# Measured transfer latencies in the scheduler, norm columns asked for from POOL's queue, and another order of inputs in the first output projection

## The chip, the cores and the metric

The kernel runs on one core of one Trainium2 chip. The metric is the device time of one execution in microseconds (us). A core has five engines that matter here, each with its own queue of instructions that it works off in order: TensorE (PE, matrix products), VectorE (DVE), ScalarE (ACT), GpSimd (POOL) and SyncE (SP), which in this kernel only asks for transfers. Engines wait for each other through semaphores.

## What is computed

A two-layer encoder over 512 positions of width 1024, in float32. Layer 0 mixes the positions with four heads of differential attention and four heads of a gated linear attention (HGRN2, both directions); layer 1 mixes them with a spatial gating unit. After each mixer comes a SwiGLU feed-forward network (FFN), and at the end a norm. The part that the change touches, from the reference:

```python
def even_mixer(h, w_in, w_out, lam, lambda_init, subln, rel_bias, lb_fwd, lb_bwd, hg_norm):
    da_q, da_k, da_v, hg_q, hg_zf, hg_zb, hg_i, hg_g = jnp.split(h @ w_in, ...)
    o_a = diff_attention(da_q, da_k, da_v, lam, rel_bias)          # heads 0 to 3
    o_a = rms_norm(o_a, subln) * (1.0 - lambda_init)
    o_b = hgrn2_bidir(silu(hg_q), hg_zf, hg_zb, hg_i, lb_fwd, lb_bwd)  # heads 4 to 7
    o_b = rms_norm(o_b, hg_norm) * silu(hg_g)
    return jnp.concatenate([o_a, o_b], axis=-1) @ w_out

# layer 0: h = h + even_mixer(rms_norm(h)); layer 1: h = h + odd_mixer(rms_norm(h))
# both:    h = h + swiglu(rms_norm(h)); at the end rms_norm(h)
```

## The kernel before

Activations lie transposed, features on the 128 partitions and the 512 positions along a row, so that a 128x512 tile is the unit of nearly all work. Each product is made of three matmuls: an operand is split into a rounded part and the rest (whi and wlo for weights, ph and pl for attention weights, vdh and vdl for values), and high x high, high x low and low x high are added. The rounded part is made by ACT, the rest by DVE, from a weight `raw` that a DMA brought.

The names that matter: `o_a` is the weighted sum of values of one attention head (four chunks of three matmuls each, from ph, pl, vdh, vdl); `pt` are transposes of the attention weights `pr`, which come from `e`, scaled on POOL; `or_b` is a gated linear head before its norm and `on` after it; `or_a` is an attention head before its norm; `g` is the gate's projection; `oe` the first output projection, with one group oe0 to oe7 for each 128 output features, and eight inputs k: attention heads for k = 0 to 3 (`oa`), gated heads for k = 4 to 7 (`ob`).

A norm over features needs, for each position, a sum over partitions. `rnorm` (lines 440 to 459) makes it: PE sums into a row (`st`), ACT copies the row (`ln`), a small DMA lays it over partitions (`ms`), POOL adds the epsilon and takes the power -1/2 (`rr`), a small DMA writes it to DRAM (`dr`), and a DMA reads it back as `R`, 128x512, the same row on each partition (256 KB). DVE then multiplies with R. There are eight such norms: gated heads b0 to b3, attention heads a0 and a1, and the norm in each of the two FFNs (f0, f1); the other norms go without the transfers. `bt` is the bias of an attention head, 448 KB.

The order of all instructions is not written by hand. `Plan.schedule` (line 110 and on) simulates five engines, with a cost for each operation and a latency after which its users may start (`LATENCY`, and 2.0 for a DMA, line 196), takes at each step the operation with the lowest priority number that is ready and has its buffers, and so emits one order. On the chip each engine works off its part of that order as it stands. All transfers are asked for by SP.

`out_proj` (line 883) makes the first two groups of the projection with all inputs but the last one, then gives them the last one, and makes the other six groups one after the other.

Of the kernel before, what the change touches and what calls it, by code (L numbers as in the profile page):

```python
# [16 lines left out]
P = 128  # L17
S = 512
# [8 lines left out]
LATENCY = 0.25  # L27
# [36 lines left out]


class Op:
    __slots__ = ("eng", "cost", "fn", "bufs", "prio", "deps", "users", "ready", "start", "table", "seq", "alt", "port")


class Plan:  # L70
# [6 lines left out]
    def buf(self, kind, name, dt=F32, shape=None):  # L77
        return Buf(self, kind, name, dt, shape)

    def op(self, eng, cost, fn, outs=(), ins=(), after=(), table=None, prio=None, alt=None, port=None):  # L80
        o = Op()
        o.port = eng == "POOL" if port is None else port
        o.alt = alt
        o.eng, o.cost, o.fn, o.table = eng, cost, fn, table
        o.seq = len(self.ops)
        if prio is None:
            prio = o.seq
            if self.base is not None:
                self.base += 1e-3
                prio = self.base  # L90
        o.prio = prio
        o.deps, o.users, o.bufs = set(after), [], set()
        for views, w in ((ins, False), (outs, True)):
            for v in views:
                if not isinstance(v, (View, Buf)):
                    continue
                b = v if isinstance(v, Buf) else v.buf
                part = None if isinstance(v, Buf) else v.part
                o.bufs.add(b)
                for q, qp, qw in b.log:  # L100
                    if (w or qw) and meets(part, qp):
                        o.deps.add(q)
                b.log.append((o, part, w))
        o.deps.discard(o)
        for b in o.bufs:
            b.left += 1
        self.ops.append(o)
        return o

    def schedule(self):  # L110
# [5 lines left out]
        table = None  # L116
        port = 0.0
# [6 lines left out]
        events = []  # L124
        n = 0
# [11 lines left out]
        while events:  # L137
# [15 lines left out]
            for e in engines:  # L153
# [39 lines left out]
                order.append(o)  # L193
                n += 1
                idle[e] = t + cost
                lat = 2.0 if e == "DMA" else LATENCY
                heapq.heappush(events, (t + cost, 2 * n, "near", o))
                heapq.heappush(events, (t + cost + lat, 2 * n + 1, "done", o))
        if len(order) != len(self.ops):
            left = [o for o in self.ops if o not in set(order)]  # L200
            raise RuntimeError("stuck: " + ", ".join(
# [6 lines left out]
def use(x):  # L208
    if isinstance(x, Buf):
        return x.ap()  # L210
    return x.get() if isinstance(x, View) else x
# [3 lines left out]
def encoder_kernel(  # L215
# [21 lines left out]
    nc = tc.nc  # L237
# [45 lines left out]
    def blk(ap, i):  # L283
        return ap[:, i * P:(i + 1) * P]

    def dma(o, i, kb, prio=None, after=()):
        return plan.op("DMA", max(kb / 360.0, 0.45), lambda: nc.sync.dma_start(use(o), use(i)), [o], [i], after=after, prio=prio)

    def inside(*xs):
        for x in xs:  # L290
# [149 lines left out]
    def rnorm(sq, n, name, kind):  # L440
        pr = buf("trn", f"sp_{name}", F32R)
        acopy(row(pr, 0), sq)
        vtt(row(pr, 1), sq, frow(pr, 0), ALU.subtract, either=True)
        ps = buf("aux", f"st_{name}")
        first = ps(lambda ap: ap[0:1])
        mms(ps, [(first, onesr[:, 0:1], row(pr, 0), True, False), (first, onesr[:, 0:1], row(pr, 1), False, True)])
        line = buf("tmp", f"ln_{name}")
        act(line(lambda ap: ap[0:1]), first, AF.Copy, scale=1.0 / n, cost=0.5)
        c, r = buf("ms", f"ms_{name}"), buf("rr", f"rr_{name}")
        dma(c, line(lambda ap: ap[0:1]), 20)  # L450
        gts(c, c, 1.0, EPS, cost=0.1)
        gtt(r, c, mhalf, ALU.pow, cost=1.1)
        dr = dp.tile([1, S], F32, name=f"dr_{name}")
        o = dma(dr.rearrange("o (p j) -> (o p) j", j=NB), r, 20)
        R = buf(kind, f"R_{name}")
        dma(R, dr.broadcast_to([P, S]), 256, after=[o])
        return R

    def operands(b, name):
# [295 lines left out]
    def da(h, q, k, base, vals):  # L755
# [3 lines left out]
        rows = um[h]  # L759
        src = bass.AP(rows.tensor, rows.offset + P - 1, [[D - 1, P], [1, 896]])  # L760
        o = plan.op("DMA", 1.3, lambda: nc.sync.dma_start(bt.ap(), src), [bt], after=[op_um] + after)
        QK, Kl = buf("huge", f"QK_{h}", F32R), buf("big", f"Kl_{h}", F32R)
        lo, hi = slice(0, 64), slice(64, 128)
        A64, V64 = 0.52, 0.6
# [118 lines left out]
    def out_proj(w, mx, order, early, name, nrm):  # L883
        group = [(buf("acc", f"{name}{d}"), weight(w[d])) for d in range(early)]
        for part in (order[:-1], order[-1:]):
            for d, (ps, wt) in enumerate(group):
                for k in part:
                    chunk2(ps, wt, k, mx[k], k == order[0], k == order[-1])
        for d, (ps, wt) in enumerate(group):
            residual(d, ps, nrm)  # L890
        for d in range(early, KC):
            ps, wt = buf("acc", f"{name}{d}"), weight(w[d])
            for k in order:
                chunk2(ps, wt, k, mx[k], k == order[0], k == order[-1])
            residual(d, ps, nrm)
# [136 lines left out]
        return gs, n, wts, one, out  # L1032

    n1 = Norm(1, "f0")
    out_proj(woe, mix, [0, 1, 4, 5, 2, 6, 7, 3], 2, "oe", n1.add)
    n2 = Norm(2, "m1")
    gs, n, wts, one, out_pair = ffn(0, n1, "a", n2.add, after=[da_end[3]])
    for dq in range(KC // 2):
# [183 lines left out]
```

## Time and profile before

| | |
|---|---|
| three runs | 1175.45, 1178.22, 1175.07 us (median 1175.45) |
| the profiled execution | 1179.28 us; its span from first to last instruction 1177.5 us |
| TensorE's mean granted clock | 0.996 of full speed |
| busy: PE, DVE, ACT, POOL | 98%, 78%, 49%, 12% of the span |

The profile is one execution. Busy time is the share of the span in which an engine runs an instruction. An engine that is not the bottleneck may stand idle at no cost; what counts here is where PE stands and which other engine, transfer or queue it stands for. The three runs lie within 3.15 us of each other.

### The profile page before, as it was taken

The numbers are of one execution on the slowest core, as the hardware profiler recorded it, in microseconds if no ns is written. First come the engines' busy times: TensorE is split into PE (matmuls) and PEld (weight loads), VectorE is DVE, ScalarE is ACT, GpSimd is POOL, SyncE is SP. The second block draws the span as 40 slices with busy tenths as digits, with TensorE's granted clock in tenths as the row PEclk, the third lists the DMA queues.
The fourth block names the chain that finished last, engine by engine and source line by source line (L and its number), as shares of the span: only waits on it lengthen the run. The fifth ranks groups of instructions, "written<-read, shape, count | busy, mean of one in ns | idle before, by whom it ended". The sixth has DMA issues, their size and how long they took to land.

```text
span 1177.5 us, 17613 instructions
## 1 busy us (share of the span) xinstructions
PE 1151.4 (98%) x7072; PEld 1029.9 (87%) x7072; DVE 915.8 (78%) x1335; ACT 577.9 (49%) x881; POOL 142.3 (12%) x146
## 2 busy tenths in 40 slices
PE   7999998999999999999999999999999999999997
PEld 5888887778889999999999888888999999999996
DVE  6776796788878987878887745659899777778775
ACT  5444546667555544444444542345555444444434
POOL 1672765223000000000000000000000000000000
PEclk9999999999999999999999999999999999999998
DMA  6612303225213322324231433331433242423202
GB/s 239 201 52 45 116 17 98 51 98 199 88 22 149 122 94 77 140 72 144 72 123 56 162 90 90 90 125 36 153 108 107 73 143 72 144 72 112 104 1 72
DMA packets 27978, 118.58 MB, mean 101 GB/s; under 512 B 5204, under 2 KB 7380, under 8 KB 19704
## 3 DMA queue, kind: packets, MB, share of 16 engines
q1 hardware_dynamic: 27896, 117.46, 29.9%
q8 instruction: 55, 0.90, 0.3%
q14 instruction: 27, 0.22, 0.1%
HBM read 115.30 MB, written 4.23 MB: 102 GB/s over the span
## 4 chain that ended last, share of the span: by engine, by line
PE 91%; DMA 4%; DVE 3%; POOL 1%; ACT 1%; issue 1%; SPq 0%; POOLq 0%; DVEq 0%; ACTq 0%
PE fo_0b L329 8%; PE fo_0a L329 8%; PE uo L329 4%; PE oe L329 4%; PE oo L329 4%; PE vo L329 4%; PE lv L655 2%; PE q L329 2%; PE zf L329 2%; PE vi L329 2%; PE zb L329 2%; PE fo_18a L329 2%; PE last L329 2%; PE g L329 2%; PE dq L329 1%; PE o_a L329 1%
## 5 line engine op out<-in xcount | busy, mean ns | idle before, releaser
L298 DVE TENSOR_TENSOR wlo<-raw,whi 128x1024 fp32r<-128x1024 f32 (+1 forms) x65 | 82.2, 1269 | 9.4 <-ACT whi L317 8.8
L298 DVE TENSOR_TENSOR lb<-comb,hb 128x1024 fp32r<-128x1024 f32 x44 | 53.7, 1221 | 38.5 <-ACT hb L317 38.5
L317 ACT CAST hb<-comb 128x1024 fp32r<-128x1024 f32 x44 | 46.1, 1048 | 61.2 <-PE pb6a L946 2.4
L298 DVE TENSOR_TENSOR la<-raw,ha 128x1024 fp32r<-128x1024 f32 x44 | 53.8, 1224 | 27.0 <-ACT ha L317 26.7
L317 ACT CAST ha<-raw 128x1024 fp32r<-128x1024 f32 x44 | 46.2, 1049 | 52.4 <-PE pa10a L946 2.4
L317 ACT CAST whi<-raw 128x1024 fp32r<-128x1024 f32 (+1 forms) x65 | 66.4, 1032 | 4.2 <-DMA raw<-we 2.6
L298 DVE TENSOR_TENSOR l<-raw,h 128x1024 fp32r<-128x1024 f32 (+1 forms) x48 | 54.5, 1135 | 16.5 <-ACT h L317 14.9
L317 ACT CAST hc<-comb 128x1024 fp32r<-128x1024 f32 x44 | 46.2, 1050 | 39.7 <-PE fo_0b L329 15.5
L317 ACT CAST h<-raw 128x1024 fp32r<-128x1024 f32 (+1 forms) x48 | 46.7, 976 | 29.4 <-PE pb6a L946 2.0
L298 DVE TENSOR_TENSOR comb<-comb,raw 128x512 f32<-128x512 f32 x88 | 60.2, 684 | 0.1
L298 DVE TENSOR_TENSOR lc<-comb,hc 128x1024 fp32r<-128x1024 f32 x44 | 53.6, 1218 | 3.8 <-ACT hc L317 3.8
L922 DVE TENSOR_TENSOR comb<-raw 128x1024 f32<-128x1024 f32 x44 | 53.6, 1218 | 0.0
L685 POOL TENSOR_TENSOR W<-W,T 128x512 f32<-128x512 f32 x37 | 47.6, 1297 | 48.2 <-PE lv L655 43.0
L310 POOL TENSOR_TENSOR rr_m<-ms_m,mhalf 128x4 f32<-128x4 f32 x2 | 4.6, 2302 | 346.0 <-DVE ms_m L306 346.0
L310 POOL TENSOR_TENSOR rr_fin<-ms_fin,mhalf 128x2 f32<-128x2 f32 x2 | 1.4, 696 | 336.7 <-DVE ms_fin L306 336.7
L329 PE MATMUL vo<-whi,x_m 128*128 128x512 f32 x128 | 40.3, 391 | 0.1
L329 PE MATMUL uo<-x_m,whi 128*128 128x512 f32 x128 | 40.1, 394 | 0.0
L329 PE MATMUL oo<-mx,whi 128*128 128x512 f32 x128 | 39.5, 390 | 0.0
L317 ACT CAST hd<-raw 128x512 fp32r<-128x512 f32 x44 | 27.4, 622 | 21.4 <-PE pa0b L946 2.0
L659 DVE COPY_PREDICATED att<-maskt,lv 128x512 f32<-128x512 uint8 x28 | 20.7, 740 | 17.1 <-PE lv L655 14.7
L648 ACT COPY km<-W 128x512 f32<-128x512 f32 x28 | 18.6, 663 | 30.5 <-POOL W L685 10.3
L655 PEld LDWEIGHTS lv<-W,km 128*128 128x128 f32 x224 | 30.5, 191 | 2.3
(2621 smaller groups left out, 4201.1 us busy)
## 6 DMA issues: line engine op xcount, KB each, us to landing
raw<-wfi SPq DMA_DIRECT2D x44, 1024.0 KB, 5.0
raw<-wfo SPq DMA_DIRECT2D x20, 1024.0 KB, 5.0
raw<-we SPq DMA_DIRECT2D x24, 512.0 KB, 5.4
raw<-wev SPq DMA_DIRECT2D x8, 512.0 KB, 5.9
raw<-woe SPq DMA_DIRECT2D x8, 512.0 KB, 4.4
raw<-wov SPq DMA_DIRECT2D x8, 512.0 KB, 4.9
raw<-wo SPq DMA_DIRECT2D x8, 512.0 KB, 3.7
raw<-woo SPq DMA_DIRECT2D x8, 512.0 KB, 3.7
```

What stands on the lines that cost most here:

```text
L298: return plan.op("DVE", cost, lambda: V.tensor_tensor(use(o), use(a), use(b), op), [o], [a, b], prio=prio, after=after, alt=alt, port=insi ...
L310: return plan.op("POOL", cost, lambda: G.tensor_tensor(use(o), use(a), use(b), op), [o], [a, b], prio=prio)
L317: return plan.op("ACT", cost, lambda: A.copy(use(o), use(a)), [o], [a], prio=prio)
L329: T.matmul(use(o), lhsT=use(l), rhs=use(r), start=s0, stop=s1)
L648: plan.op("ACT", 0.52, lambda km=km, s=s: A.copy(km.ap().rearrange("p (n two s) -> p n two s", two=2, s=s), mixed(1, 0, S, s)(W.ap())), [k ...
L655: T.matmul(blk(ps.ap(), b), lhsT=blk(km.ap(), b), rhs=mixed(0, b * P, P, s)(W.ap()), start=True, stop=True)
L659: plan.op("DVE", 0.6, lambda ps=ps, li=li: V.copy_predicated(att.ap().rearrange("p (b c) -> p b c", b=NB), maskt[:, li:li + 1].broadcast_t ...
L685: return lambda: eng.tensor_tensor(view(W.ap()), view(W.ap()), fn(TT.ap()), ALU.mult)
L922: plan.op("DVE", 1.14, lambda: V.tensor_tensor(comb.ap()[:, 0:2], raw.ap()[:, 0:1].broadcast_to([P, 2, S]), raw.ap()[:, 1:3], ALU.add), [c ...
```

## The change

Three things are changed. Each operation of the plan has a latency of its own (`lat`), which is as before except for four kinds of transfers: ms 1.5, dr 1.0, R 4.5 and bt 5.0 in place of 2.0. The eight R transfers are issued by `nc.gpsimd` (POOL's queue) instead of `nc.sync` (SP's). And the first output projection takes its inputs in the order 4, 5, 6, 7, 0, 1, 2, 3.

```diff
 class Op:
-    __slots__ = ("eng", "cost", "fn", "bufs", "prio", "deps", "users", "ready", "start", "table", "seq", "alt", "port")
+    __slots__ = ("eng", "cost", "fn", "bufs", "prio", "deps", "users", "ready", "start", "table", "seq", "alt", "port", "lat")
...
+        o.lat = 2.0 if eng == "DMA" else LATENCY
...
-                lat = 2.0 if e == "DMA" else LATENCY
-                heapq.heappush(events, (t + cost + lat, 2 * n + 1, "done", o))
+                heapq.heappush(events, (t + cost + o.lat, 2 * n + 1, "done", o))
...
-    def dma(o, i, kb, prio=None, after=()):
-        return plan.op("DMA", max(kb / 360.0, 0.45), lambda: nc.sync.dma_start(use(o), use(i)), [o], [i], after=after, prio=prio)
+    def dma(o, i, kb, prio=None, after=(), q=nc.sync):
+        return plan.op("DMA", max(kb / 360.0, 0.45), lambda: q.dma_start(use(o), use(i)), [o], [i], after=after, prio=prio)
...
-        dma(c, line(lambda ap: ap[0:1]), 20)
+        dma(c, line(lambda ap: ap[0:1]), 20).lat = 1.5
...
         o = dma(dr.rearrange("o (p j) -> (o p) j", j=NB), r, 20)
+        o.lat = 1.0
         R = buf(kind, f"R_{name}")
-        dma(R, dr.broadcast_to([P, S]), 256, after=[o])
+        dma(R, dr.broadcast_to([P, S]), 256, after=[o], q=G).lat = 4.5
...
         o = plan.op("DMA", 1.3, lambda: nc.sync.dma_start(bt.ap(), src), [bt], after=[op_um] + after)
+        o.lat = 5.0
...
-    out_proj(woe, mix, [0, 1, 4, 5, 2, 6, 7, 3], 2, "oe", n1.add)
+    out_proj(woe, mix, [4, 5, 6, 7, 0, 1, 2, 3], 2, "oe", n1.add)
```

What the change does to the order is seen at three places. In the rows below, the number right behind a name is that of the head, block or weight, and the last number that of the buffer.

The first place is DVE's queue around the norm of gated head b2, whose R is R_b2; on2 is the normed head, and pl_0 and vdl belong to attention head 0. Before:

```order
L298 TENSOR_TENSOR pl_0_1670<-pt2_0_1592,ph_0_1661 128x512
L298 TENSOR_TENSOR wlo25_1686<-raw25_1412,whi25_1677 128x1024
L302 SCALAR_TENSOR_TENSOR on2_1695<-or_b2_1530,colt_81,R_b2_1664 128x512
L659 COPY_PREDICATED att3_1282<-maskt_87,lv64_3_1679 128x512
L298 TENSOR_TENSOR pl_0_1670<-pt3_0_1603,ph_0_1661 128x512
L302 SCALAR_TENSOR_TENSOR vdl_1724<-vd0_1397,rr_m0_295,vdh_1709 128x512
L771 TENSOR_TENSOR QK_1_1717<-dqr1_1459,QK_1_1717 64x512
L302 SCALAR_TENSOR_TENSOR vdl_1724<-vd1_1403,rr_m0_295,vdh_1709 128x512
L302 SCALAR_TENSOR_TENSOR vdl_1724<-vd2_1476,rr_m0_295,vdh_1709 128x512
L302 SCALAR_TENSOR_TENSOR vdl_1724<-vd3_1545,rr_m0_295,vdh_1709 128x512
```

The same place of DVE's queue in the order of the change:

```order
L298 TENSOR_TENSOR pl_0_1674<-pt2_0_1611,ph_0_1662 128x512
L298 TENSOR_TENSOR pl_0_1674<-pt3_0_1615,ph_0_1662 128x512
L660 COPY_PREDICATED att3_1315<-maskt_87,lv32_3_1683 128x512
L686 TENSOR_TENSOR W_3_1201<-W_3_1201,T_3_1181 128x16x32
L302 SCALAR_TENSOR_TENSOR vdl_1708<-vd0_1395,rr_m0_295,vdh_1698 128x512
L302 SCALAR_TENSOR_TENSOR vdl_1708<-vd1_1402,rr_m0_295,vdh_1698 128x512
L302 SCALAR_TENSOR_TENSOR vdl_1708<-vd2_1469,rr_m0_295,vdh_1698 128x512
L302 SCALAR_TENSOR_TENSOR on2_1727<-or_b2_1515,colt_81,R_b2_1656 128x512
L302 SCALAR_TENSOR_TENSOR vdl_1708<-vd3_1523,rr_m0_295,vdh_1698 128x512
L298 TENSOR_TENSOR wlo26_1741<-raw26_1572,whi26_1725 128x1024
```

All four pl_0 and three of the four vdl now stand ahead of on2, and a weight's split (wlo26) behind the last vdl; before, the last pl_0 and all four vdl stood behind on2.

The second place is POOL's queue around the norm of gated head b3 (ms_b3, rr_b3, R_b3), with e2_1 and e3_1 of attention head 1. Before:

```order
L313 TENSOR_SCALAR ms_b3_1896<-ms_b3_1896 128x4
L313 TENSOR_SCALAR e2_1_1877<-e2_1_1877,rs2_1_1918 128x512
L310 TENSOR_TENSOR rr_b3_1943<-ms_b3_1896,mhalf_84 128x4
L313 TENSOR_SCALAR e3_1_1907<-e3_1_1907,rs3_1_1969 128x512
L779 MEMSET Kl_2_1998 64x512
L780 MEMSET Kl_2_1998 64x512
L313 TENSOR_SCALAR e0_2_2071<-e0_2_2071,rs0_2_2110 128x512
```

The same place of POOL's queue in the order of the change:

```order
L313 TENSOR_SCALAR e2_1_1896<-e2_1_1896,rs2_1_1934 128x512
L313 TENSOR_SCALAR ms_b3_1929<-ms_b3_1929 128x4
L310 TENSOR_TENSOR rr_b3_1961<-ms_b3_1929,mhalf_84 128x4
L781 MEMSET Kl_2_1972 64x512
L782 MEMSET Kl_2_1972 64x512
L287 DMA R_b3_1994<-dr_b3_107 128x512
L313 TENSOR_SCALAR e3_1_1936<-e3_1_1936,rs3_1_2008 128x512
```

R_b3 is now asked for here, and e3_1 stands behind it; e2_1 went ahead of ms_b3.

The third place is PE's queue at the end of attention: the transposes of the last part of attention head 3 (pr3_3), and o_a3. Before:

```order
L817 MATMUL pt0_3_2412<-ident_82,pr3_3_2497 128x128
L817 MATMUL pt1_3_2442<-ident_82,pr3_3_2497 128x128
L817 MATMUL pt2_3_2458<-ident_82,pr3_3_2497 128x128
L817 MATMUL pt3_3_2462<-ident_82,pr3_3_2497 128x128
L329 MATMUL g3_2492<-x_m02_139,whi31_2303 128x512 x2
L329 MATMUL g3_2492<-x_m02_139,wlo31_2326 128x512
L329 MATMUL g3_2492<-x_m03_147,whi31_2303 128x512 x2
L329 MATMUL g3_2492<-x_m03_147,wlo31_2326 128x512
L329 MATMUL g3_2492<-x_m04_168,whi31_2303 128x512 x2
L329 MATMUL g3_2492<-x_m04_168,wlo31_2326 128x512
L329 MATMUL o_a3_2531<-ph_3_2508,vdh_1709 128x512
```

The same place of PE's queue in the order of the change:

```order
L819 MATMUL pt0_3_2485<-ident_82,pr3_3_2567 128x128
L819 MATMUL pt1_3_2487<-ident_82,pr3_3_2567 128x128
L819 MATMUL pt2_3_2532<-ident_82,pr3_3_2567 128x128
L819 MATMUL pt3_3_2539<-ident_82,pr3_3_2567 128x128
L329 MATMUL o_a3_2585<-ph_3_2576,vdh_1698 128x512
L329 MATMUL o_a3_2585<-pl_3_2580,vdh_1698 128x512
L329 MATMUL o_a3_2585<-ph_3_2576,vdl_1708 128x512
```

The three chunks of the gate's projection g3 that stood between the transposes and o_a3 are gone from there; they stand further ahead. Some 40 rows further on, in the order of the change, the last chunks of oe0, oe1 and oe2 follow each other and then comes oe3; before, oe0 and oe1 ended together, all eight chunks of oe2 followed, and then oe3. On DVE the two additions h0<-oe0 and h0<-oe1 and then the split wlo35, which oe3 needs, follow each other in both orders.

## Rows read from the trace of the kernel before

**Rows 1.** The page's first part: busy us, share of the span, instructions.

```profile
PE 1151.4 (98%) x7072; PEld 1029.9 (87%) x7072; DVE 915.8 (78%) x1335; ACT 577.9 (49%) x881; POOL 142.3 (12%) x146
```

**Rows 2.** Timeline of PE, 183 to 206 us: start us, us, operation, [idle before <-releaser].

```profile
183.93 0.63 PE L329 MATMUL st_b<-sp_b,onesr 128*1 128x512 f32 x2
...
201.15 0.48 PE L329 MATMUL o_a<-ph,vdh 128*128 128x512 f32 x1
...
205.05 0.79 PE L329 MATMUL o_a<-ph,vdl 128*128 128x512 f32 x1 [3.19 <-DVE vdl L302]
```

**Rows 3.** Timeline of DVE, 201 to 205 us.

```profile
201.89 1.25 DVE L302 SCALAR_TENSOR_TENSOR on<-or_b,colt,R_b 128x512 f32<-128x512 f32 x1 [5.00 <-DMA R_b<-dr_b]
...
204.27 0.73 DVE L302 SCALAR_TENSOR_TENSOR vdl<-vd,rr_m,vdh 128x512 fp32r<-128x512 f32 x1
```

**Rows 4.** Busy time by window: engines, PEclk, DMA share, GB/s.

```profile
205.00:208.40 3.40, 3.35 (x8) 2.35 (x9) 3.34 (x5) 1.03 (x2) 0.00 (x0) 0.51 0.00 0
```

**Rows 5.** Timeline of PE, 236 to 258 us.

```profile
236.70 0.50 PE L329 MATMUL o_a<-ph,vdh 128*128 128x512 f32 x1 [1.51 <-DVE pl L298]
...
257.67 0.50 PE L329 MATMUL o_a<-ph,vdh 128*128 128x512 f32 x1 [1.15 <-DVE pl L298]
```

**Rows 6.** Timeline of DVE, readers of R at three more places.

```profile
235.30 0.75 DVE L302 SCALAR_TENSOR_TENSOR on<-or_b,colt,R_b 128x512 f32<-128x512 f32 x1 [1.17 <-DMA R_b<-dr_b]
...
256.27 0.75 DVE L302 SCALAR_TENSOR_TENSOR or_a<-or_a,subln,R_a 128x512 f32<-128x512 f32 x1 [1.33 <-DMA R_a<-dr_a]
...
838.79 0.68 DVE L298 TENSOR_TENSOR y0b<-y0b,R_f 128x512 f32<-128x512 f32 x1
```

**Rows 7.** Timeline of SP's queue: issues of dr and R.

```profile
191.82 0.33 SPq L287 DMA_DIRECT2D dr_b<-rr_b  x1
...
195.25 0.33 SPq L287 DMA_DIRECT2D R_b<-dr_b  x1
...
226.78 0.32 SPq L287 DMA_DIRECT2D dr_b<-rr_b  x1
...
230.89 0.32 SPq L287 DMA_DIRECT2D R_b<-dr_b  x1
...
251.35 0.33 SPq L287 DMA_DIRECT2D R_a<-dr_a  x1
...
833.90 0.33 SPq L287 DMA_DIRECT2D R_f<-dr_f  x1
```

**Rows 8.** DMA issues by group: KB each, median us from issue to landing.

```profile
R_b<-dr_b SPq DMA_DIRECT2D x4, 256.0 KB, 5.2
...
dr_b<-rr_b SPq DMA_DIRECT2D x4, 2.0 KB, 1.4
```

**Rows 9.** Timeline of POOL, 189 and 224 us.

```profile
189.13 1.68 POOL L313 TENSOR_SCALAR e<-e,rs 128x512 f32<-128x512 f32 x1
...
224.02 0.70 POOL L313 TENSOR_SCALAR e<-e,rs 128x512 f32<-128x512 f32 x1
```

**Rows 10.** Timeline of PE, 300 to 302 us: one chunk of the first output projection.

```profile
300.98 0.62 PE L329 MATMUL oe<-oa,whi 128*128 128x512 f32 x2
...
301.66 0.62 PE L329 MATMUL oe<-oa,whi 128*128 128x512 f32 x2
```

**Rows 11.** Timeline of PE, ACT and DVE, 281 to 283 us.

```profile
281.37 0.60 PE L817 MATMUL pt<-ident,pr 128*128 128x128 f32 x4
...
281.67 2.06 ACT L317 CAST ph<-pt 128x512 fp32r<-128x512 f32 x4 [0.25 <-PE pt L817]
...
282.31 2.47 DVE L298 TENSOR_TENSOR pl<-pt,ph 128x512 fp32r<-128x512 f32 x4
```

**Rows 12.** Timeline of DVE, 300 to 303 us.

```profile
300.50 1.37 DVE L298 TENSOR_TENSOR h<-h,oe 128x512 f32<-128x512 f32 x2 [2.68 <-PE oe L329]
301.79 1.22 DVE L298 TENSOR_TENSOR wlo<-raw,whi 128x1024 fp32r<-128x1024 f32 x1
```

**Rows 13.** Waits of PE: us in total, times, longest.

```profile
PE pb2b L946 <- DVE y1b L298: 0.5, 1, 0.5
```

## The prediction

> **What bounds the kernel now.** I began with the page's first part: TensorE (PE) is busy for 1151.4 us, 98% of the span [rows 1]. So a change of order can only give back or add time in which PE stands. The waits by engine lead to three places in the attention stage, all behind one kind of transfer, the column R that a norm spreads over 128 partitions. I read each on PE's timeline and then on VectorE's (DVE).
>
> Stall A: PE has nothing for 3.19 us before the first o_a product that needs vdl [rows 2]. DVE made that vdl only at 204.27, since ahead of it in its queue stood on<-or_b,R_b, which waited 5.00 us for R_b and ran at 201.89 [rows 3]. After the stall the granted clock was 0.51, the 1.2 GHz level, for 3.40 us [rows 4]; at 2.4 GHz that work takes about half as long, so 1.7 us went there. Stall A costs about 4.9 us. Stalls B and C are PE's 1.51 and 1.15 us before o_a [rows 5]: pl, which o_a needs, stood on DVE behind `on` (1.17 us for R_b) and behind or_a (1.33 us for R_a) [rows 6]. Together the three are some 7.6 us, the most that the change can remove.
>
> Next I followed R backwards on SP's queue. At A the small transfer dr_b was asked for at 191.82 and R_b at 195.25, and `on` started at 201.89: 3.4 us and 6.6 us. At B it was 226.78, 230.89 and 235.30: 4.1 and 4.4 us. At C, R_a took 4.9 us (251.35 to 256.27) [rows 3, 6, 7]. The median of R_b is 5.2 us [rows 8].
>
> **The change part by part.** The new latencies issue nothing; they only move rows. Eight R transfers go from SP's queue to POOL's. No other instruction is added.
>
> *What R costs from POOL's queue.* No transfer of before was issued there, so this is the open price. Call L the time from when R may be asked for until its reader starts. Lower bound: the fastest R of SP, 4.4 us. Upper bound: the slowest, 6.6, plus the 1.0 us by which POOL's work is drawn out at times: the same e<-e,rs takes 0.70 us in one row and 1.68 in another [rows 9]; so 7.6. I take 5.8: the median of 5.2, and 0.6 on top, between no stretch and the whole.
>
> The Trainium skill, page "SBUF — State Buffer", in its part on the three doors (the "DVE blocks DMA" trap), says that the descriptors of a DMA issued by GpSimd cannot be written while DVE holds a port pair that the two share, and tells of a DMA of about 620 ns that took 3100 ns so. By that figure L would be near 7.7, and the sum below some 8 us worse. The trace agrees that POOL is held up at times, by 1.0 us [rows 9].
>
> *Stall A.* By the order, DVE now makes pl and three of the four vdl before `on`, and only the last vdl after it. But PE also reaches o_a sooner. Before, st_b started at 183.93 and o_a at 201.15, 17.2 us [rows 2]. Of what stands between, 6 of 54 matmuls of 128x512 went elsewhere (three take 0.68 us [rows 10], so 1.4) and 4 small transposes (about 0.4: four in 0.6 [rows 11]); the group pa has moved behind, and a group lv of its size into the middle of o_a. The last vdl is wanted three chunks (2.0) and two matmuls (0.45) after o_a's start: 17.9 us after st_b. It is there after 11.3 (183.93 to 195.25), L, then `on` and vdl, 1.25 and 0.73 [rows 3]: 13.3 + 5.8 = 19.1. So PE still waits 1.2 us, too short for me to expect the slow clock, which followed a stall of 3.19. Gain 4.9 - 1.2 = 3.7; at L = 4.4 the whole 4.9, at 7.6 it is 1.9.
>
> *Stall B.* `on` still stands ahead of pl. L takes the place of 4.4: +1.4. On POOL an e (0.70 [rows 9]) no longer stands between ms_b and rr_b: -0.7. For dr_b, 4.1 here and 3.4 at A, I take 3.4: -0.7. And PE has less to do meanwhile: 3 projection and 4 score matmuls fewer stand between st_b and o_a, 7 x 0.227 = 1.6, which becomes waiting. Sum: 1.6 us lost (0.2 at L = 4.4, 3.4 at 7.6). Part of it will show before the transposes pt: e3, from which they come, stands on POOL behind R's request, and that waits for dr_b.
>
> *Stall C.* L takes the place of 4.9: +0.9; PE has 3 matmuls more in between: -0.7. Lost: 0.2 (from a gain of 1.2 to a loss of 2.0).
>
> *End of attention, two new waits.* Before, three g chunks stood between the last four transposes and o_a; now o_a follows at once. The transposes start at 281.37, ACT's ph at 281.67, DVE's first pl at 282.31, and one pl of the four in 2.47 takes 0.62 [rows 11]: ready 1.56 us after the transposes' start, with PE through them in at most 0.6, and sooner since ends overlap. Lost: 1.2 (1.0 to 1.3). Then the projection: oe0, oe1 and oe2 now end together, one chunk of 0.68 us each [rows 10], and oe3 follows. Its wlo stands on DVE behind two additions h<-h,oe (1.37 for both) and takes 1.22 [rows 12]. The second addition waits for oe1's end; from there it is about 0.7 + 1.2 us, and PE covers 0.68 (oe2) and 0.45 (two matmuls of oe3): 0.8, and with the two hand-overs I take 1.0 lost (0.7 to 1.4). Before, oe2 stood whole between oe1 and oe3 and hid this split: that cover is gone. The first chunk of oe2 needs its own split earlier than before: 0, at most 1.2.
>
> *The FFN norms.* Their order is as before. In layer 1, R_f was asked for at 833.90 and its reader y0b started at 838.79, 4.9 us [rows 6, 7], and PE already waits 0.5 us for y1b [rows 13], which stands on DVE behind what follows y0b. So L - 4.9 = 0.9 us is lost (0 to 2.7). In layer 0 I take 0, and at most as much as in layer 1.
>
> **Sum:** -3.7 + 1.6 + 0.2 + 1.2 + 1.0 + 0.9 = +1.2. The profiled execution took 1179.28, so 1180.5 in one of that kind; on the median of the runs, 1175.45, it gives 1176.6. The profiled one lies 3.8 above the median, and the three runs differ by 3.15: what can be told from no change is about 0.3%, 3.5 us.
>
> **The rivals.**
> *Faster.* On a queue of its own R no longer stands among weight loads and lands in 4.4 us, and dr_b in its median of 1.4 [rows 8]. Then A is gone (-4.9); B gives 1.6 - 1.4 - 2.0, at most its whole 1.5; C its 1.15; layer 1 loses nothing; the end of attention still costs 2.2. Sum -5.3: 1170.1. With dr_b at 3.4 it is -3.6, just at the bound. For it: R took 4.4 at one place and 6.6 at another, so what travels beside it matters. Against it: the loads still travel at the same time.
> The Trainium skill, page "DMA: Bandwidth & Descriptors", section "SWDGE vs HWDGE vs iDMA", speaks for this rival: requests of the two kinds feed different queues inside a DMA engine, which takes them in turn. No run so far shows it.
> *Slower.* R from POOL lands late. Each us of L costs about 4: one each at A, B, C and layer 1; later layer 0 joins in. The sum passes +3.5 from L = 6.4. At L = 7.2 it is 1.2 + 1.4 x 4 + 1.0 for layer 0 = +7.8: 1183.2. For it: POOL's stretched row [rows 9]. Against it: it must hold at four places.
> *It doesn't do what it says.* The weight loads that SP held back while it waited to ask for R now leave at once behind dr_b; the R_b of stall A alone meets them and lands after 7.6, A's gain shrinks by 1.8, and if the slow clock comes back too, by 3.5: +4.7, 1180.1 (+3.0 without the clock). The 6.6 us of that R, the longest of the rows, speaks for it.
>
> **How the numbers follow.** Forecast (no change that can be told) 0.43, faster rival 0.17, slower rival 0.27, A unchanged 0.13, half of it within 0.3%. That makes faster 0.17, same 0.49, slower 0.34. The range, 1171.0 to 1183.5, reaches from near the faster rival to just past the slower one and leaves out the far ends of both. The forecast's own range is 1173 to 1179.
>
> **What would show it.** A: PE's wait for vdl near 1.2 us and no slow clock behind it; 3 us with 0.51 after it is the third rival. L itself: from R's request on POOL to its reader. B: waits at pt and o_a that sum to about 3. End of attention: o_a waiting for ph or pl by 1.2, oe waiting for wlo by 1.0. Layer 1: PE's waits before pb1b or pb2b longer by 0.9. I am wrong if L lies outside 4.4 to 7.6, or if PE waits somewhere that I have not named.

## The result and the profile after

The change makes the kernel slower: 1188.18 us at the median of 6 runs, 1177.62 for the kernel before on the same chip (6 runs), ratio 1.0087 with a 95% interval of 1.0073 to 1.0102. The medians lie 10.6 us apart. The profiled execution took 1187.36 us, 8.1 more than that of before; what the traces below account for is the 8.1, and no trace shows where the other 2.5 lie. Of the changed kernel's profiled span of 1185.6 us PE is busy for 1154.7, which answers to [rows 1]: 3.3 us more busy, though it runs the same 7072 matmuls, and 4.8 us more idle. One execution further below, of a kernel with the old list of inputs, ran at a granted clock of 0.85 throughout and took 1258.61 us; it enters no ratio.

The page's first part of the changed kernel:

```profile
PE 1154.7 (97%) x7072; PEld 1032.2 (87%) x7072; DVE 917.4 (77%) x1335; ACT 580.3 (49%) x883; POOL 144.7 (12%) x154
```

Where PE stands now, by the waits of PE in the changed kernel behind the start of the program (us in total, times, longest); the row of [rows 13] is there still, with 0.6:

```profile
PE pb1b L948 <- DVE c1b L298: 3.1, 1, 3.1
PE pt L819 <- DVE pr L302: 2.9, 2, 2.2
PE o_a L329 <- DVE pl L298: 2.2, 2, 1.1
PE pb1a L948 <- DVE c1a L298: 2.0, 1, 2.0
...
PE pa0a L948 <- DVE xlp_f L477: 1.0, 1, 1.0
PE oe L329 <- DVE wlo L298: 0.8, 1, 0.8
```

Stall A is not in the list. DVE's timeline of the changed kernel at that place shows why; it answers to [rows 3]:

```profile
198.20 2.06 DVE L302 SCALAR_TENSOR_TENSOR vdl<-vd,rr_m,vdh 128x512 fp32r<-128x512 f32 x3
200.53 0.75 DVE L302 SCALAR_TENSOR_TENSOR on<-or_b,colt,R_b 128x512 f32<-128x512 f32 x1 [0.28 <-DMA R_b<-dr_b]
201.20 0.75 DVE L302 SCALAR_TENSOR_TENSOR vdl<-vd,rr_m,vdh 128x512 fp32r<-128x512 f32 x1
```

Three vdl stand ahead of `on`, and `on` waits 0.28 us for R_b instead of 5.00. The first reader of the last vdl stands on PE at 202.73, without a wait, and the half clock of [rows 4] is gone from here.

It came back at two other places. PE busy and granted clock in two windows of the changed kernel:

```profile
252.20:255.60 3.40, 3.40 (x12) 2.71 (x11) 0.46 (x2) 0.59 (x2) 0.00 (x0) 0.50 0.53 215
361.40:364.80 3.40, 3.40 (x19) 3.40 (x18) 2.19 (x4) 1.34 (x3) 0.00 (x0) 0.51 0.24 48
```

The first stretch begins just after PE stood 2.22 us before pt at 251.61, the second after it stood 2.03 us before pb1a at 359.99. At the 1.2 GHz level each 3.40 us hold about half the work, so each costs some 1.7 us; one such stretch before, two now, is 1.7 of the 3.3 us by which PE is busier.

**The longest wait.** In layer 1's FFN the norm's transfers are asked for by two engines. SP's queue and POOL's timeline in the changed kernel:

```profile
835.70 0.33 SPq L287 DMA_DIRECT2D dr_f<-rr_f  x1
836.13 1.51 SPq L287 DMA_DIRECT2D raw<-wfo  x1
837.69 0.91 SPq L287 DMA_DIRECT2D raw<-wfi  x2
838.70 0.39 SPq L287 DMA_DIRECT2D raw<-wfo  x1
```

```profile
838.84 0.62 POOL L287 DMA_DIRECT2D R_f<-dr_f  x1 [3.16 <-DMA dr_f<-rr_f]
```

SP no longer waits for dr_f, since R is not its business any more. It goes on at once and has four weight loads under way when POOL, which does wait for dr_f, asks for R_f. What then happens is seen in DVE's timeline and in PE's:

```profile
842.03 1.22 DVE L298 TENSOR_TENSOR lb<-comb,hb 128x1024 fp32r<-128x1024 f32 x1
846.62 0.69 DVE L298 TENSOR_TENSOR y0b<-y0b,R_f 128x512 f32<-128x512 f32 x1 [3.37 <-DMA R_f<-dr_f]
847.23 0.41 DVE L298 TENSOR_TENSOR c1b<-c1b,pb1b 128x256 f32<-128x256 f32 x1
```

```profile
847.70 0.39 PE L948 MATMUL pb1b<-xhp_f,hc 128*128 128x256 f32 x1 [3.13 <-DVE c1b L298]
```

R_f's reader starts 7.8 us after the request (838.84 to 846.62), against 4.9 in the kernel before [rows 6, 7]; c1b stands behind that reader, and PE behind c1b. The packets by queue show which transfer held which. Queue 1 carries what SP asks for, queue 0 what POOL asks for (packets, MB, share of the 16 engines). From 838.8 to 842.8 us, the first 4.0 us after the request:

```profile
q1 hardware_dynamic: 234, 1.32, 88.3%
```

And from 842.8 to 846.6 us:

```profile
q1 hardware_dynamic: 157, 1.16, 76.9%
q0 software_dynamic: 80, 0.26, 23.8%
```

In the first four microseconds not one packet of R_f moved while 234 packets of weights did; then all its 80 moved beside the loads' rest. With the loads beside it dr_f is slower too: from its request to R's it is 3.1 us now (835.70 to 838.84) and was 2.6 in the kernel before (831.31 to 833.90). The Trainium skill, page "DMA: Bandwidth & Descriptors", section "SWDGE vs HWDGE vs iDMA", which the prediction cites, has the two kinds of queues served in turn. By these rows R got no turn for 4 us and shared the engines with the loads after that; the rows do not show when R was ready to move, so how far they are against the page stays open.

**The same transfer with nothing in its way.** At 213.58 us POOL asks for R_a when no load is outstanding. The DMA issues of that moment (KB, us to landing), the packets up to 215.4, and the busy time of the engines until it landed:

```profile
R_a<-dr_a POOLq DMA_DIRECT2D x1, 256.0 KB, 3.6
```

```profile
q0 software_dynamic: 17, 0.07, 18.0%
```

```profile
213.58:217.20 3.62, 3.62 (x17) 3.00 (x16) 1.91 (x7) 3.08 (x8) 1.32 (x2) 1.00 0.32 72
```

3.6 us is less than any R of before took to land (4.4 to 6.6), though SP's R can be as quick: in the run with SP and a latency of 4.0 below, one landed after 3.0. Here the first packets moved 1.2 us after the request, so of the 4.0 us in layer 1 some 2.8 are left for what stood in the way (an estimate from these two times). The page "SBUF — State Buffer" of the Trainium skill, in the trap that the prediction cites, has DVE hold up a transfer that GpSimd issues. These rows alone do not rule it out: DVE was busy for 0.33 of the 1.22 us ahead of the first packets here, and for 2.60 of the 3.96 us in layer 1. Against it as the main cause speak that the request held POOL for 0.62 us at both places, and the run with R on ACT's queue below, where POOL does not issue R and R_f is as late.

By group the changed kernel's issues answer to [rows 8] (KB, median us to landing):

```profile
R_b<-dr_b POOLq DMA_DIRECT2D x4, 256.0 KB, 4.9
...
R_f<-dr_f POOLq DMA_DIRECT2D x2, 256.0 KB, 7.6
...
dr_b<-rr_b SPq DMA_DIRECT2D x4, 2.0 KB, 2.5
```

The median of R_b hides the matter (4.9, it was 5.2); R_f's 7.6 and dr_b's 2.5 (it was 1.4) show it.

### The profile page after: what moved, and what is told of

Read it like the earlier page. It is cut to its first block, busy times and chain, and to the rows that moved or that the text cites. A ratio compares the mean times of both kernels' runs of the same rounds, so it can differ in the third digit from the quotient of the medians.

```text
span 1185.6 us, 17608 instructions
## 1 busy us (share of the span) xinstructions
PE 1154.7 (97%) x7072; PEld 1032.2 (87%) x7072; DVE 917.4 (77%) x1335; ACT 580.3 (49%) x883; POOL 144.7 (12%) x154
## 4 chain that ended last, share of the span: by engine, by line
PE 89%; DVE 4%; DMA 4%; ACT 1%; issue 1%; POOL 1%; POOLq 0%; SPq 0%; DVEq 0%; ACTq 0%
PE fo_0b L329 8%; PE fo_0a L329 8%; PE uo L329 4%; PE oo L329 4%; PE vo L329 4%; PE lv L656 2%; PE q L329 2%; PE zf L329 2%; PE vd L329 2%; PE vi L329 2%; PE zb L329 2%; PE fo_18a L329 2%; PE last L329 2%; PE g L329 1%; PE dq L329 1%; DMA R_f<-dr_f 1%
## 5 line engine op out<-in xcount | busy, mean ns | idle before, releaser
L298 DVE TENSOR_TENSOR l<-raw,h 128x1024 fp32r<-128x1024 f32 (+1 forms) x48 | 54.5, 1136 | 18.2 <-ACT h L317 16.6
L660 DVE COPY_PREDICATED att<-maskt,lv 128x512 f32<-128x512 uint8 x28 | 20.7, 739 | 18.7 <-PE lv L656 17.4
```

The lines of the kernel that those rows point to most:

```text
L298: return plan.op("DVE", cost, lambda: V.tensor_tensor(use(o), use(a), use(b), op), [o], [a, b], prio=prio, after=after, alt=alt, port=insi ...
L660: plan.op("DVE", 0.6, lambda ps=ps, li=li: V.copy_predicated(att.ap().rearrange("p (b c) -> p b c", b=NB), maskt[:, li:li + 1].broadcast_t ...
```

## The experiments

Theory 1 is that R is late where weight loads are asked for ahead of it, and that they are asked for ahead because SP no longer waits for dr. Its rivals: theory 2, POOL's queue is slow by itself; theory 3, the new order costs the time, and R has little to do with it. Each ratio is to the kernel before, measured beside it on the same chip, with its 95% interval.

**R on SP's queue, all else as in the change.** The orders of PE, DVE, ACT and POOL are those of the change, but for R's requests.

```diff
-        dma(R, dr.broadcast_to([P, S]), 256, after=[o], q=G).lat = 4.5
+        dma(R, dr.broadcast_to([P, S]), 256, after=[o]).lat = 4.5
```

> All of the change but its queue: R is asked for by SP again, right behind dr, so SP holds the weight loads back as before; PE, DVE, ACT and POOL have the change's order. Theory 1 (loads that SP now asks for ahead of R hold R up): R_f starts its reader 5 to 5.7 us after the request instead of 7.6, PE's waits in the two FFNs fall from 2.0 and 3.1 us to under 0.5, the 2.2 us before pt in attention go too; the end of attention keeps its 3 us of waits. Time 1180 to 1183. Theory 2 (POOL's queue is slow by itself, above all beside DVE) expects the same of this run. Theory 3 (the new order costs the time, not R): about 1187, within 2 us of the change.

Measured: 1177.94 us, ratio 0.9995 (0.9981 to 1.0008). Theory 3 falls: with the same order of work the whole loss is gone, and more of it than theory 1 had said (1180 to 1183). SP's queue in this kernel, layer 1:

```profile
830.76 0.33 SPq L287 DMA_DIRECT2D dr_f<-rr_f  x1
833.39 0.33 SPq L287 DMA_DIRECT2D R_f<-dr_f  x1
833.77 0.42 SPq L287 DMA_DIRECT2D raw<-wfo  x1
```

The loads stand behind R_f now, which lands after 4.6 us. PE's wait before pb1b is gone, that before pb1a falls from 2.0 to 0.7, and no stretch at the half clock is left in the trace. What stays, beside that, is the change's own end of attention; PE's timeline of this kernel:

```profile
281.66 0.44 PE L819 MATMUL pt<-ident,pr 128*128 128x128 f32 x2 [0.68 <-DVE pr L302]
282.27 1.16 PE L819 MATMUL pt<-ident,pr 128*128 128x128 f32 x6 [0.17 <-DVE mn L804]
289.16 0.50 PE L329 MATMUL o_a<-ph,vdh 128*128 128x512 f32 x1 [1.07 <-DVE pl L298]
305.06 0.50 PE L329 MATMUL oe<-ob,wlo 128*128 128x512 f32 x1 [0.79 <-DVE wlo L298]
```

These are the same four waits as in the changed kernel, so they come with the order, not with the queue.

**R on POOL's queue, but SP held back.** Right behind dr, SP copies 16 bytes of it elsewhere, so that it waits for dr as before and the loads leave later. The copy is extra work; R stays with POOL.

```diff
-        dma(R, dr.broadcast_to([P, S]), 256, after=[o], q=G).lat = 4.5
+        g = dp.tile([1, 4], F32, name=f"hold_{name}")
+        src = dr.broadcast_to([P, S])
+        def both():
+            G.dma_start(use(R), src)
+            nc.sync.dma_start(g, dr[0:1, 0:4])
+        plan.op("DMA", 256 / 360.0, both, [R], [], after=[o]).lat = 4.5
```

> R stays on POOL's queue, but SP also copies 16 bytes of dr to DRAM right behind dr, so that SP waits until dr has landed before it asks for the next weight loads, as it did before the change. Theory 1: R and the loads are now asked for at about the same time, R_f is there after 4 to 5.5 us, FFN waits of PE under 0.7 us; time 1180 to 1183. Theory 2: R_f still takes 7 us or more, PE still waits 2 and 3 us in the FFNs, time 1187 to 1190. Theory 3: about 1187.

Measured: 1180.52 us, ratio 1.002 (1.0007 to 1.0032), so most of the 0.87% is gone with R still on POOL. R_f lands after 5.3 and 6.2 us. Layer 1 by SP's queue and POOL:

```profile
832.03 0.62 SPq L462 DMA_DIRECT2D hold_f<-dr_f  x1
832.71 0.43 SPq L287 DMA_DIRECT2D raw<-wfo  x1
```

```profile
832.54 0.62 POOL L461 DMA_DIRECT2D R_f<-dr_f  x1 [3.19 <-DMA dr_f<-rr_f]
```

Loads are asked for from 0.17 us behind R on. That is still close: R's first packets moved 2.5 us after the request, between the 1.2 with nothing in the way and the 4.0 behind four loads, and PE stands 1.69 us before pb1b here, where it stood 3.13, and 0.9 before pb1a. So the time came out as theory 1 had it, but R_f and the waits are somewhat longer than it said. Stall C shrinks as well, with R_a and the e behind it still on POOL:

```profile
246.43 0.62 POOL L461 DMA_DIRECT2D R_a<-dr_a  x1 [1.71 <-DMA dr_a<-rr_a]
```

POOL goes on 1.7 us after dr_a was asked for (244.75 to 246.43), and PE stands 0.83 us before pt.

**R on ACT's queue.** A third queue, whose requests are of SP's kind (hardware_dynamic) and which POOL has no part in; the loads are still ahead.

```diff
-        dma(R, dr.broadcast_to([P, S]), 256, after=[o], q=G).lat = 4.5
+        dma(R, dr.broadcast_to([P, S]), 256, after=[o], q=A).lat = 4.5
```

> R is asked for from ACT's queue, neither POOL's nor SP's; the weight loads leave SP ahead of it as in the change. ACT's own work waits behind the request until dr has landed, which adds waits of its own, so the time alone tells little. Theory 1: the two R_f take 7 us or more, as on POOL's queue, and PE waits 2 us and more in each FFN. Theory 2: they take about 5, as on SP's queue.

Measured: 1189.71 us, ratio 1.0095 (1.0071 to 1.012). R_f lands after 9.0 and 8.1 us. Theory 2 falls: R_f is late without POOL's queue, and PE stands 3.2 us before pb1a and 3.0 before pb1b. The time by itself says less, since ACT's own work stands behind the request here (3.38 us in layer 1). ACT asks for layer 1's R_f at 838.63, behind three loads, and the packets of the 4.4 us after that (838.6 to 843) are, by queue, with 10 being ACT's:

```profile
q1 hardware_dynamic: 244, 1.36, 89.6%
q10 hardware_dynamic: 15, 0.03, 1.9%
```

15 packets of R among 244 of the loads, and none of the 15 before 842.5, 3.9 us after the request.

**Only the two R of the FFNs back on SP.**

```diff
-        dma(R, dr.broadcast_to([P, S]), 256, after=[o], q=G).lat = 4.5
+        dma(R, dr.broadcast_to([P, S]), 256, after=[o], q=nc.sync if name[0] == "f" else G).lat = 4.5
```

> The change, with R of the two FFN norms alone asked for from SP's queue, behind its wait for dr; the six R of the attention stages stay on POOL's queue. Theory 1 (R is late where weight loads are asked for ahead of it): the two FFN stalls (2.2 and 3.3 + 0.7 us in the changed kernel) fall to about those of the change with all R on SP (0.8 and 0.7), R_f lands 5.0 to 5.6 us after its request, and the half clock behind the first FFN stall (361.4 to 364.8, some 1.7 us of work lost) does not come; the pt stall of 2.4 us at 251 stays, and the half clock behind it. That is 4.7 + 1.7 = 6.4 us of the 10.5: about 1181.5, ratio 1.002 to 1.005. Rival 2 (POOL's queue costs the same everywhere, the FFN places are only where it shows): the stalls behind the six attention R would have to grow or others appear where it has slack no longer, and the time stays over 1185, ratio above 1.006.

Measured: 1181.66 us, ratio 1.0021 (1.001 to 1.0032), as theory 1 had it. R_f lands after 5.4 and 4.7 us, and there is no half clock behind layer 0. So the two FFN norms are where most was lost: 0.66 of the 0.87%. What is left, beside the end of attention, is stall C and the half clock behind it (0.53 from 252.70 to 256.10). POOL's timeline and PE's in this kernel:

```profile
249.47 0.62 POOL L287 DMA_DIRECT2D R_a<-dr_a  x1 [3.26 <-DMA dr_a<-rr_a]
250.14 1.36 POOL L313 TENSOR_SCALAR e<-e,rs 128x512 f32<-128x512 f32 x2
```

```profile
252.10 0.66 PE L819 MATMUL pt<-ident,pr 128*128 128x128 f32 x4 [2.33 <-DVE pr L302]
```

Here it is not R that is late for its reader first, but the two e behind R's request: POOL may not go on until dr_a has landed, 3.26 us, DVE's pr needs the e, and PE's transposes need pr. In the kernel before, SP did that waiting. And dr_a itself is slow: SP asked for it at 246.24, with two loads right behind, and POOL goes on 3.2 us later, where it was 1.7 with SP held back.

**The queue alone, on the kernel before.** Old latencies, old order of inputs, R on POOL's queue.

```diff
-        dma(R, dr.broadcast_to([P, S]), 256, after=[o])
+        dma(R, dr.broadcast_to([P, S]), 256, after=[o], q=G)
```

> The kernel before with R on POOL's queue and nothing else: old latencies, old order of inputs. Theories 1 and 2: the FFNs cost 5 us more as in the change (R_f 7.6), stall A shrinks or grows with R_b; time 1181 to 1185. Theory 3: within 2 us of before.

Measured: 1193.26 us, ratio 1.0125 (1.0105 to 1.0146). The queue alone costs more than the whole change, and 8 us more than the upper end that theories 1 and 2 gave. PE's longest waits in this kernel, behind the start of the program:

```profile
PE o_a L329 <- DVE pl L298: 3.6, 2, 3.2
PE pb1b L946 <- DVE c1b L298: 3.5, 1, 3.5
PE o_a L329 <- DVE vdl L302: 3.2, 1, 3.2
```

Stall A (vdl, 3.2) is there, with the waits of the queue beside it; two more of over 2 us are pa1a for c1a (2.4) and pt for pr (2.2). The trace has four stretches at the half clock, some 20 us together, against one of 3.40 us before, and PE is busy for 1158.4 us, 7.0 more than before. That is what the expectation had not counted.

**The latencies alone, and the list of inputs alone.** The first has R on SP and the old list; the second is the kernel before with the new list.

```diff
-    out_proj(woe, mix, [0, 1, 4, 5, 2, 6, 7, 3], 2, "oe", n1.add)
+    out_proj(woe, mix, [4, 5, 6, 7, 0, 1, 2, 3], 2, "oe", n1.add)
```

> The change's four latencies alone: R on SP's queue, the output projection's list of inputs as before. Theory 1: the stall A of 3.2 to 3.4 us at 201.9 is removed by the latencies alone, since nothing of it hangs on the queue or the list: it is absent here too. The end of attention keeps the stalls that the change has there (o_a about 1.2, and pt), because the latencies make them; the time is within 0.2% of the change with R on SP (ratio 0.9995): 0.998 to 1.0015. Rival 3 (the list of inputs gives what is lost at the end of attention, or takes it away): this run is off that one by over 1.5 us, with the difference between 280 and 310 us of the trace.

> The list of inputs of the first output projection alone, [4, 5, 6, 7, 0, 1, 2, 3]; latencies and queue as before. Theory 1: nothing ahead of the end of attention changes, so the stall A stays at 3.2 to 3.4 us, the FFN stalls at 0.4 + 1.1 + 0.6 and 0.7; the time is that of the kernel before within 1.5 us, ratio 0.9985 to 1.0015. Rival 3: the list moves the last inputs into the way of the projection that waits for wlo, and 1 us or more is lost between 280 and 310 us: ratio over 1.001.

Measured: latencies alone 1178.0 us, ratio 0.999 (0.9977 to 1.0003); list alone 1179.68 us, ratio 1.0 (0.999 to 1.0009). Stall A is gone with the latencies and there with the list; PE's timeline with the list alone:

```profile
205.31 0.66 PE L329 MATMUL o_a<-ph,vdl 128*128 128x512 f32 x1 [3.19 <-DVE vdl L302]
```

What the latencies gain at A they lose in part at the end of attention (both oe) and in layer 0 (pb1a, 0.9, which did not wait before); o_a for pl is what is left of stalls B and C. PE's waits with the latencies alone, behind the start:

```profile
PE o_a L329 <- DVE pl L298: 1.9, 2, 1.7
PE oe L329 <- ACT oa L317: 1.6, 1, 1.6
...
PE oe L329 <- DVE wlo L298: 0.8, 1, 0.8
```

The expectation held in the time; one detail did not: at the end of attention PE stands 1.6 us for oa, not 1.1 for pl. The list decides which of the two it is.

**A true number for POOL's R.** R from POOL with a latency of 5.0, which with the 0.71 us that the planner gives the transfer itself is the mean of the eight R measured.

```diff
-        dma(R, dr.broadcast_to([P, S]), 256, after=[o], q=G).lat = 4.5
+        dma(R, dr.broadcast_to([P, S]), 256, after=[o], q=G).lat = 5.0
```

> The change as it is, R from POOL's queue, with R's latency at 5.0 in place of 4.5: with the planner's 0.71 for the transfer that is 5.7 us, the mean of the eight R in the changed kernel (3.6 to 7.7). Theory 1 (R of the FFN norms is late because weight loads are asked for ahead of it, and the FFN stages have no other work to put there): R_f still lands 7 us and more after its request, the FFN stalls of 2.2 and 3.3 + 0.7 us stay, and only the pt stall of 2.4 us with the half clock behind it can go: ratio 1.005 to 1.009. Rival (a true number in the plan is enough, wherever the transfer is asked for): the stalls go with it, ratio 0.998 to 1.002.

Measured: 1191.6 us, ratio 1.0101 (1.0085 to 1.0118), above what either side expected. The rival falls. Theory 1 is right only in part: R_f lands after 7.5 us in both FFNs and the stall before pb1b stays (3.4 us), but that in layer 0 falls to 0.6, so there the new order did find other work. The pt stall of 2.2 at C is gone; one of 2.1 stands at the end of attention instead, and the new order has waits of its own before lv (1.3), sp_a (1.4) and st_a (0.8). Two half-clock stretches of 6.8 us each (286.2 and 849.4 on) follow. One mean did not help here, where the true value runs from 3.6 to 7.7 by what is under way; which of the new waits come from the number and which from the order is not shown.

**R on SP with a latency of 4.0.** The mean of the eight R in the first experiment was 4.8 us, near to 4.0 with the 0.71 that the planner gives the transfer itself.

```diff
-        dma(R, dr.broadcast_to([P, S]), 256, after=[o], q=G).lat = 4.5
+        dma(R, dr.broadcast_to([P, S]), 256, after=[o]).lat = 4.0
```

> The change with R on SP's queue and its latency set to 4.0 in place of 4.5. With the planner's 0.71 us for the transfer itself that makes 4.7 us from request to reader, against a mean of 4.8 measured in the change with R on SP (3.85 to 5.40) and 5.2 before this edit. Theory A (what is left at the end of attention comes from numbers that are too large, so that work is planned ahead of work that was ready): the stalls A, pt 0.8 + 0.3, o_a 1.2 and oe 0.95 go in whole or in good part: 1.5 to 5 us under the change with R on SP, ratio to the kernel before 0.995 to 0.998. Theory B (the planner's numbers are near enough, and what is left is set by the work itself): ratio 0.998 to 1.0005, stalls as there.

Measured: 1176.8 us, ratio 0.9981 (0.9972 to 0.999), which is faster than both kernels, though against the same with 4.5 (0.9981 to 1.0008) the intervals overlap. By time it lies at the edge of the two theories, just inside B's range; by the stalls it is theory A: A and C and those of o_a and oe are gone, but for 0.7 at pt. PE's waits in this kernel, behind the start and the end of the program:

```profile
PE s L799 <- DVE mn L804: 1.5, 1, 1.5
PE pa0a L948 <- DVE lb L298: 0.8, 1, 0.8
PE pt L819 <- DVE pr L302: 0.7, 1, 0.7
```

**The same with bt's latency as before (2.0).**

```diff
-        o.lat = 5.0
+        o.lat = 2.0
```

> The change with R on SP's queue, R's latency 4.0 and the latency of the bias transfer (bt) left at 2.0, as before; measured in the changed kernel bt takes some 5.4 us. Theory A (the bias is needed late enough that its number only shifts which work is planned first): the same as with 5.0, ratio 0.997 to 0.999. Theory B (a number too small by over 3 us makes work stand behind the bias): a stall of 1 to 3 us at the first reader of bt, some 225 to 260 us, ratio 0.999 to 1.002.

Measured: 1177.06 us, ratio 0.9985 (0.9976 to 0.9994). The bias's number does not matter here, though a bt takes 5.4 us.

**The same with the old list of inputs, twice.** The stalls are read from the second run.

```diff
-    out_proj(woe, mix, [4, 5, 6, 7, 0, 1, 2, 3], 2, "oe", n1.add)
+    out_proj(woe, mix, [0, 1, 4, 5, 2, 6, 7, 3], 2, "oe", n1.add)
```

> The change with R on SP's queue, R's latency at 4.0, and the output projection's list of inputs as before. The list alone moved nothing measurable (1.000), and neither did taking it out beside R's latency of 4.5 (0.9990 against 0.9995). Theory A (the latency of 4.0 gives the gain of 0.9981, by taking away the stalls around the end of attention): the ratio is 0.997 to 0.999, pt, o_a and oe stalls between 280 and 310 us stay away. Theory B (the list gives it, since with it the last inputs come first): the stalls of 1 us each come back there, ratio 0.999 to 1.001.

> The kernel with R on SP's queue at a latency of 4.0 and the old list of inputs once more, since its first profiled execution ran at a granted clock of 0.85 throughout, so that no stall could be read from it, and its ratio (1.0001) was over that with the new list (0.9981). If the list matters beside 4.0, the ratio is 0.9992 to 1.001 again, and 1.5 to 2.5 us of stalls stand between 200 and 310 us that the one with the new list does not have. If the first measurement was off, the ratio is 0.997 to 0.999 and the stalls are those of the one with the new list.

Measured: 1178.69 us, ratio 1.0001 (0.9992 to 1.001), and 1178.91 us, ratio 1.0005 (0.9996 to 1.0014). So the latency of 4.0 alone gives nothing, and neither did the list alone; the two together give some 0.2%. By time it is what theory B expected, but its stalls of 1 us at the end of attention did not come back, and of the 1.5 to 2.5 us expected between 200 and 310 us 0.9 did. Where the 0.2% goes is not settled: two waits stand in the second run's profile that the new list's does not have (pa0a for xlp_f, 1.0 us, and s for QK, 0.9), but the two profiled spans are 1175.6 and 1175.7 us.

## Why the prediction was wrong

The forecast was no change that can be told (1176.6); measured was 1.0087. The terms, in the profiled executions, with what the prediction gave and what the traces show:

| place | predicted | measured | how read |
|---|---|---|---|
| A | -3.7 | -4.9 | wait 3.19 and half clock, both gone |
| B | +1.6 | -0.4 | 1.51 before, 1.09 now, both at o_a |
| C | +0.2 | +2.8 | 1.15 before; 2.22 at pt and 1.7 of half clock now |
| end of attention | +2.2 | +2.7 | o_a 1.07, oe 0.79; and pt 0.69 + 0.17, not named |
| layer 1 | +0.9 | +3.2 | 3.13 + 0.58 against 0.5 |
| layer 0 | 0 | +4.2 | 2.03 at pb1a, 1.7 of half clock, 0.5 at its start |
| sum | +1.2 | +7.6 | of 8.1 between the two profiled executions (10.6 between the medians) |

**The step that failed** is the price of R from POOL's queue: one L for all places, 5.8 us, the median of SP's R and a stretch of POOL on top. From request to reader the trace has 5.8 at A, 4.0 at B, 6.4 at C, 7.7 in layer 0 and 7.8 in layer 1. The prediction said that it would be wrong if L lay outside 4.4 to 7.6 or PE waited somewhere that it had not named; both came true. The hit at A is luck: three transfers (two weights and a bias, 191.95 to 193.18) had been asked for ahead of R_b there, which the price knew nothing of. It missed in both FFNs, where loads that stood behind R now leave ahead of it, and it missed there because the prediction looked at how slow POOL can be and not at what SP does with the time it no longer spends waiting. The experiments show the latter: SP as R's issuer, or SP held back with R still on POOL, gives all or most of the time back, and R on ACT, behind the same loads, is as late.

The mechanism itself stands in the prediction, in the third rival, but at one place only, stall A; there R_b landed after 5.8 us, and PE saw nothing of it, because three vdl had moved ahead of R's reader. Which loads stand behind R on SP's queue could be read at every place, and I read it only for A.

**Layer 0** was taken as 0. The row to look at was DVE's in the kernel before:

```profile
353.63 0.69 DVE L298 TENSOR_TENSOR y0a<-y0a,R_f 128x512 f32<-128x512 f32 x1 [1.26 <-DMA R_f<-dr_f]
```

DVE stood for R there already, and c1a, which PE waits for now, is the third row behind. The same row after the change:

```profile
357.17 0.69 DVE L298 TENSOR_TENSOR y0a<-y0a,R_f 128x512 f32<-128x512 f32 x1 [3.11 <-DMA R_f<-dr_f]
```

DVE's wait is 1.85 us longer, and PE now stands 2.03. The half clock behind it, another 1.7, was in no case of the prediction but that of A. And "their order is as before" was not quite so: the stage now starts with pa0a, which stands 0.95 us for xlp_f; its three waits at the start sum to 2.17 us against 1.69.

**C** failed for another reason than L. For B the prediction said that e stands on POOL behind R's request and that this waits for dr; for C it counted L alone. POOL's timeline of the changed kernel:

```profile
248.97 0.62 POOL L287 DMA_DIRECT2D R_a<-dr_a  x1 [3.14 <-DMA dr_a<-rr_a]
```

The wait for dr_a took 3.14 us, and by way of e and pr it reached PE before R did. With only the FFNs' R back on SP this stall stays at 2.33; with R_a on SP too it is gone. But POOL's waiting is only part of it: with SP held back POOL waits for dr_a as well, only 1.71 us, and PE stands 0.83. So C, too, comes in good part from the loads that SP now asks for at once: with two of them right behind, POOL went on 3.1 us after dr_a's request, and 1.7 without them.

**A** came out better than forecast: dr_b was asked for sooner after st_b, so R's request came 10.2 us after it (184.53 to 194.74) and not 11.3, `on` took 0.75 us and not 1.25, and the last vdl was there at 17.4 us where PE wanted it at 18.2. **B** is mis-sized mainly by L, 4.0 in place of 5.8: with 4.0 its sum is -0.2, and -0.4 was measured. **The end of attention** is right in both named waits (1.07 for 1.2, 0.79 for 1.0); the pt wait of 0.7 that comes with it was missed.

**The slower rival** had the sign and, for the profiled executions, nearly the size (+7.8 at an L of 7.2, against 8.1), but not the places: it wanted R late at A, B, C and layer 1 alike. A and B were not late for PE, and layer 0 and the half clock, which it priced at 1.0 and 0, made up for them. **The faster rival** had the right price for a queue with nothing in its way (3.6 us, less than its 4.4), and at the FFNs there was something in the way.

## What to carry to other kernels

A wait on a queue that only issues transfers also holds back what is queued behind it. Before moving a transfer off such a queue, read what stands behind it there: that is what will leave first, and the moved transfer lands behind it; the small transfer that it waits for can be late by the same loads (3.1 us in place of 1.7 at stall C). And the engine that takes over the request takes over the wait: whatever compute stands behind it there is late by that. A planner's latency should be measured on the queue that the transfer will use, with its neighbours; where the neighbours made it anything from 3.6 to 7.7 us, the mean was no help (1.0101). What the measured number gave on SP's queue was small: 0.2%, and only together with the new list of inputs.

## What the runs showed of the hardware

A 256 KB transfer asked for by POOL landed in 3.6 us with nothing outstanding, less than any of SP's in the kernel before (4.4 to 6.6; 3.0 in the run with SP and 4.0), and in 7.7 us behind four loads. Its first packets moved 1.2 us after the request with nothing outstanding, 2.5 with loads asked for from 0.17 us later on, 4.0 behind four loads in layer 1 and 4.7 behind two in layer 0, although it had a queue of its own; from ACT's queue, behind three loads, it was 3.9. In what order the DMA engines serve the queues was not settled: once R's packets began, they moved beside those of the loads, so the transfers are not served whole in the order of their requests, and for the first 2.5 to 4.7 us none of R's moved at all.

PE's clock fell to the 1.2 GHz level for 3.40 us after waits of 2.22 and 2.03 us in attention and in the FFN of layer 0, but not after the longest, 3.13 us in layer 1. At that same place it did fall with R on ACT's queue (after a wait of 3.01 us, at 848.9) and with R's latency at 5.0 (849.4 on, within a wait of 3.42 us that ended at 850.86). Why the one and not the others is open.
